# A Conformer trunk step on one core: the convolution stage's layer norms written in order with their sums on VectorE, and the last feed-forward block's first norm among the output projection's products

## The chip, the core and the metric

The kernel runs on one core of a Trainium2 chip. The metric is device time in microseconds (us) of one execution. A core has TensorE (PE, matrix products into PSUM), VectorE (DVE), ScalarE (ACT), GpSimd (POOL), and SyncE (SP), which issues most DMA transfers. Each engine runs its own queue in order and waits on semaphores for the others.

## The reference

One step of a hybrid trunk with a residual stream of 1024 features and 640 frames: 512 of a new stream and 8 x 16 of running streams. Layer 0 is a Conformer convolution module and a feed-forward block, layer 1 is chunked attention to a shared K/V and a feed-forward block, and a final RMS norm follows. Everything is float32. The parts that matter here:

```python
def layer_norm(x, g, b):
    xf = x.astype(jnp.float32)
    mu = jnp.mean(xf, axis=-1, keepdims=True)
    var = jnp.mean(jnp.square(xf - mu), axis=-1, keepdims=True)
    y = (xf - mu) * lax.rsqrt(var + EPS)
...
def swiglu_ffn(h, g, w_in, w_out):
    a, b = jnp.split(rms_norm(h, g) @ w_in, 2, axis=-1)
    return h + (jax.nn.silu(a) * b) @ w_out
...
    y = lax.conv_general_dilated(
...
    y = jax.nn.silu(layer_norm(y, ln_g, ln_b))
    return h + y @ w_pw2 + b_pw2, full[:, -CONV_HIST:]
...
            h = h + o @ w_o[j]
        h = swiglu_ffn(h, norm_ffn[l], w_ffn_in[l], w_ffn_out[l])
```

The convolution is depthwise, 31 frames wide.

## The kernel before

**Layout.** Features lie on the 128 partitions, in 8 tiles (KT), and frames along the free axis, in two groups of 320 (g = 0 and 1; 256 and 384 around attention). A float32 product is made of three fast ones: each operand is split into a high and a low part (ACT rounds the high part, VectorE subtracts), and PE multiplies high by high, low by high and high by low (mm3, L179 to L181). Weights come by DMA into `raw` and are split in the same way (wsplit, `whi` at L152, `wlo` at L156).

**Convolution stage.** It follows PLAN, a string of steps. `a`, `b`, `D` and so on to `F` are products of a channel block with its gate. `S`, `A` and `B` are depthwise convolutions of a block on PE (conv_pe, L804): 32 matmul instructions for each of the three parts of a block's frames; four of them, one `tg`, are called a step below. `q` is a block whose convolution is 31 taps, each an ACT product (`cvt`, L777) and a POOL add (`ca`, L780); further blocks are taps on VectorE (L769). Convolutions leave PSUM by a copy to `y` on ACT (to_y, L738). The inputs of S and A (`xa`) go from `gall`, which the gates on VectorE write (L724, L730), by DMA to DRAM and back, shifted (conv_shift, conv_read). The steps `n0` and `n1` are the layer norms of the two groups, LN0 and LN1 (conv_ln, L823), `w0` and `w1` the second pointwise product (pw2, L848) of the groups, whose results are added to `h` on VectorE (L862).

**Norms.** Sums over features are column sums on PE: a matmul of a data tile with a column of 1/1024 (colmean, L216). The first LCUT or SQCUT of the eight tiles are added up beforehand (L207, on POOL or VectorE) and go to PE as one; the others go to PE singly. A small reduction (L220), eps (L250) and a power of -1/2 on POOL (L257) follow, and PE spreads the result over the partitions by the identity (spread, L228). LN0 adds five of eight tiles for its mean, and none of its squares; LN1 adds five and eight.

**Feed-forward.** ffn() (L299) makes seven products where a plain scheme has eight; its first three hidden tiles are plain products (std) of the input's quarters: X11 and X21 for the first half of the frames, XT4 and X22 for the second. Each half has its norm: stats(half) (L551) makes squares (ACT, L188), sums, the spread and a copy on ACT (L554), xnorm multiplies (VectorE, L558), xput splits (ACT L337, VectorE L338). The products stand at L404. FFN0 is the block of layer 0, FFN1 that of layer 1.

**Output projection.** halves(r) (L1221) makes the products of the last heads: for each half of the frames eight tiles of six products, in PSUM tiles `mm` and `am` by turns, each added to `h` on VectorE (L1230).

**What sets the order.** A scheduler orders each engine's instructions by priority; tc.high_priority lifts what is inside, and behind(...) and tc.issue_after(...) make an instruction stand after a given one. What is written without such ties may be moved forward into gaps.

## Time and profile before

| | |
|---|---|
| median of 3 runs | 1491.54 us (1490.59 to 1494.51) |
| profiled execution | 1494.89 us |
| its span | 1493.1 us |
| mean granted TensorE clock | 0.988 |
| PE, VectorE, ACT, POOL busy | 97%, 75%, 51%, 22% of the span |

The profiled execution is one run and lies 3.35 us above the median of the runs, so sums are made against 1494.89 and carried over as differences. Times in the rows are us from the start of the span; `[3.00 <-ACT y L738]` means that the engine was idle for 3.00 us and that ACT's instruction at line 738 ended it. A matmul on f32 operands (convolutions, column sums, spreads) leaves two records for each instruction.

### The profile page before, as it was taken

Reading aid. Unit: us, or ns where it says so; the run is one execution under the profiler, and the core shown is the slowest. Engines: PE = TensorE matmul, PEld = TensorE weight load, DVE = VectorE, ACT = ScalarE, POOL = GpSimd, SP = SyncE. Lnnn points to the kernel's source line nnn. Section 1 sums busy time; section 2 is a strip of 40 time slices with the busy share of each in tenths; the row PEclk is TensorE's granted clock in tenths of the full one; section 3 lists DMA queues with packets and bytes.
Section 4 is the critical chain, followed back from the end, with each engine's and each line's share of the span. In section 5 each row is a group of like instructions: output and inputs, shape, how many; then the busy total and the mean of one; then the engine's idle time right before and its main releaser. Section 6 shows DMA issues by size and latency. Waiting matters only on the chain.

```text
span 1493.1 us, 28157 instructions
## 1 busy us (share of the span) xinstructions
PE 1443.9 (97%) x10998; PEld 1377.0 (92%) x10998; DVE 1125.9 (75%) x2494; ACT 757.4 (51%) x1620; POOL 325.5 (22%) x376
## 2 busy tenths in 40 slices
PE   5998999999999999999999999999999999999997
PEld 5997789999999999999988898878999999999997
DVE  5788546799788788766867668576788888788754
ACT  3666246464554554444655355443454455465443
POOL 5789322011111111013222111012001111111101
PEclk9999999999999999999999999999899999999998
DMA  7167514034544544424555554452024544544512
GB/s 238 67 169 199 117 57 140 31 101 121 156 110 118 153 112 116 145 86 157 195 175 193 178 193 163 142 186 78 29 75 118 148 117 115 151 117 108 157 58 71
DMA packets 66661, 192.57 MB, mean 129 GB/s; under 512 B 12000, under 2 KB 30176, under 8 KB 58080
## 3 DMA queue, kind: packets, MB, share of 16 engines
q1 hardware_dynamic: 52736, 161.10, 33.2%
q0 software_dynamic: 13504, 29.37, 9.7%
q8 instruction: 86, 1.41, 0.4%
q14 instruction: 47, 0.39, 0.1%
q10 hardware_dynamic: 288, 0.31, 0.1%
HBM read 179.14 MB, written 11.61 MB: 128 GB/s over the span
## 4 chain that ended last, share of the span: by engine, by line
PE 81%; POOL 6%; DVE 6%; ACT 4%; DMA 1%; issue 1%; POOLq 0%; DVEq 0%; ACTq 0%
PE mm L404 48%; PE mm L179 8%; PE mm L180 7%; PE mm L181 7%; POOL ca L780 5%; PE mm L818 2%; PE w L216 2%; PE am L1154 1%; PE w L1170 1%; PE am L1137 1%; ACT whi L144 1%; PE am L1201 1%; DVE wlo L338 1%; ACT whi L152 1%; DVE hid L558 1%
## 5 line engine op out<-in xcount | busy, mean ns | idle before, releaser
L404 PE MATMUL mm<-XH,whi 128*128 128x320 f32 x896 | 276.0, 311 | 1.1 <-ACT t L414 1.0
L404 PE MATMUL mm<-XH,wlo 128*128 128x320 f32 x896 | 277.0, 310 | 0.0
L404 PE MATMUL mm<-XL,whi 128*128 128x320 f32 x896 | 274.7, 309 | 0.0
L337 ACT ACTIVATE whi<-raw 128x512 fp32r<-128x512 f32 (+2 forms) x280 | 169.4, 613 | 146.2 <-PE mm L404 114.5
L179 PE MATMUL mm<-xh,whi 128*128 128x320 f32 (+2 forms) x640 | 201.0, 316 | 4.2 <-ACT xh L168 2.6
L338 DVE TENSOR_TENSOR wlo<-raw,whi 128x512 fp32r<-128x512 f32 (+2 forms) x280 | 184.9, 668 | 22.8 <-ACT whi L337 21.6
L180 PE MATMUL mm<-xh,wlo 128*128 128x320 f32 (+2 forms) x640 | 199.7, 313 | 0.6 <-DVE wlo L156 0.6
L181 PE MATMUL mm<-xl,whi 128*128 128x320 f32 (+2 forms) x640 | 196.8, 312 | 0.0
L404 PE MATMUL mm<-hid,whi 128*128 128x320 f32 x732 | 172.0, 310 | 2.9 <-DVE hid L338 2.6
L404 PEld LDWEIGHTS mm<-XH,whi 128*128 128x128 f32 x896 | 168.4, 189 | 2.1 <-ACT t L414 2.1
L404 PEld LDWEIGHTS mm<-XH,wlo 128*128 128x128 f32 x896 | 168.7, 188 | 0.0
L404 PEld LDWEIGHTS mm<-XL,whi 128*128 128x128 f32 x896 | 167.9, 188 | 0.0
L404 PEld LDWEIGHTS mm<-hid,whi 128*128 128x128 f32 x732 | 124.8, 188 | 5.8 <-DVE hid L338 3.7
L179 PEld LDWEIGHTS mm<-xh,whi 128*128 128x128 f32 x640 | 121.5, 190 | 7.4 <-ACT xh L168 3.1
L180 PEld LDWEIGHTS mm<-xh,wlo 128*128 128x128 f32 x640 | 121.7, 190 | 1.0 <-DVE wlo L156 0.8
L181 PEld LDWEIGHTS mm<-xl,whi 128*128 128x128 f32 x640 | 120.6, 189 | 0.4 <-issue 0.2
L404 PE MATMUL mm<-hid,wlo 128*128 128x320 f32 x366 | 112.9, 308 | 0.0
L404 PE MATMUL mm<-XH,shi 128*128 128x320 f32 x344 | 107.2, 312 | 3.2 <-ACT XH L337 3.2
L404 PE MATMUL mm<-XL,shi 128*128 128x320 f32 x344 | 106.8, 312 | 1.3 <-DVE XL L338 1.3
L404 PE MATMUL mm<-XH,slo 128*128 128x320 f32 x344 | 106.9, 311 | 0.0
L383 POOL DMA_DIRECT2D s<-in_w_in x38 | 22.0, 579 | 388.8 <-DVE wlo L338 208.6
L780 POOL TENSOR_TENSOR ca<-ca,cvt 128x512 f32<-128x512 f32 x60 | 91.4, 1524 | 15.0 <-ACT cvt L777 8.0
(245 smaller groups left out, 3389.1 us busy)
## 6 DMA issues: line engine op xcount, KB each, us to landing
raw<-in_w_in SPq DMA_DIRECT2D x38, 1024.0 KB
s<-in_w_in POOLq DMA_DIRECT2D x76, 256.0 KB, 4.2
raw<-in_w_os SPq DMA_DIRECT2D x24, 768.0 KB
cache<-in_ck SPq DMA_DIRECT2D x32, 512.0 KB
cache<-in_cv SPq DMA_DIRECT2D x32, 512.0 KB
raw<-in_w_pw SPq DMA_DIRECT2D x12, 1024.0 KB
s<-in_w_os POOLq DMA_DIRECT2D x48, 192.0 KB, 3.6
raw<-in_w_kq SPq DMA_DIRECT2D x8, 1024.0 KB
```

What stands on the lines that cost most here:

```text
L144: nc.scalar.activation(out=hi[:, a:b], in_=raw[:, a:b], func=AF.Copy, scale=gain)
L152: nc.scalar.activation(out=hi[:, a:b], in_=raw[:, a:b], func=AF.Copy)
L179: nc.tensor.matmul(ps, wh, xh, start=(i == 0), stop=False)
L180: nc.tensor.matmul(ps, wl, xh, start=False, stop=False)
L181: end = nc.tensor.matmul(ps, wh, xl, start=False, stop=(i == last))
L216: nc.tensor.matmul(st[:, 512 + t * w + k:513 + t * w + k], s[:, a:a + P], onec, start=True, stop=True)
L337: nc.scalar.activation(out=hi, in_=src, func=AF.Copy)
L338: put_end[0] = nc.vector.tensor_tensor(out=lo, in0=src, in1=hi.bitcast(F32), op=sub).ins
L383: nc.gpsimd.dma_start(s1, src[:, 2 * n:3 * n])
L404: last = nc.tensor.matmul(pt, wt, v, start=(first and k == i == 0), stop=(k == n - 1 and i == 2), skip_group_check=True)
L780: nc.gpsimd.tensor_tensor(out=acc, in0=acc, in1=pr, op=ALU.add)
L818: nc.tensor.matmul(pt[32 * q:32 * q + 32, 0:n], w4[0:r, 4 * tg + q, :], mv, start=(tg == 0), stop=(tg == 7))
```

## The change

**Convolution stage.** The step `n` writes LN0 in pieces among the last convolutions, each tied behind the other: mean sums, one step of B5, the spread; then subtractions, squares and adds against 12 steps, the variance sums, two steps, the spread, and the rest (staged_ln, GAPS). All adds of LN0 and LN1 are on VectorE. LN0's mean adds seven of eight tiles (LCUT) and its variance all eight squares. LN1 (step `m`) is written before w0 and tied behind LN0's last add. The first two tiles of pw2 take turns by k. QHELD takes the last two taps of channel block 3 from where they stood and issues them after the next gate (step `e`).

On PE, from LN0's mean sums on (L216 and L221 are column sums, L228 and L233 spreads, L818 and L832 convolutions of B5, B6 and B7), before:

```order
L216 MATMUL w_233_1985<-onec,acc_1986 128x1 x3
L216 MATMUL w_233_1985<-onec,y_102 128x1 x7
L818 MATMUL mm_2101<-xb_1371,w_177_1242 32x320 x3
L216 MATMUL w_233_1985<-onec,y_102 128x1 x2
L818 MATMUL mm_2101<-xb_1371,w_177_1242 32x320 x18
L228 MATMUL w_233_1985<-ident,mst_2003 128x128 x3
L818 MATMUL mm_2101<-xb_1371,w_177_1242 32x320 x11
L818 MATMUL mm_2140<-xb_1574,w_193_1377 32x320 x13
L216 MATMUL w_237_2018<-onec,sql_2017 128x1 x24
L818 MATMUL mm_2140<-xb_1574,w_193_1377 32x320 x19
L818 MATMUL mm_2174<-xb_2135,w_212_1614 32x320 x3
L228 MATMUL w_237_2018<-ident,rst_239_2054 128x128 x3
```

and with the change:

```order
L221 MATMUL w_233_1985<-onec,acc_1986 128x1 x3
L221 MATMUL w_233_1985<-onec,y_102 128x1 x3
L832 MATMUL mm_2002<-xb_1365,w_175_1236 32x320 x4
L233 MATMUL w_233_1985<-ident,mst_1999 128x128 x3
L832 MATMUL mm_2002<-xb_1365,w_175_1236 32x320 x28
L832 MATMUL mm_2070<-xb_1568,w_191_1371 32x320 x20
L221 MATMUL w_238_2019<-onec,acc_2022 128x1 x3
L832 MATMUL mm_2070<-xb_1568,w_191_1371 32x320 x8
L233 MATMUL w_238_2019<-ident,rst_243_2096 128x128 x3
L832 MATMUL mm_2070<-xb_1568,w_191_1371 32x320 x4
L832 MATMUL mm_2156<-xb_2065,w_210_1608 32x320 x32
L221 MATMUL w_255_2191<-onec,acc_2192 128x1 x3
```

The 24 sums of single squares (`sql`) became three, and each of the norm's steps stands at a fixed place. Further on, LN1's last spread stood 39 products ahead of the first product of w1; now it is four.

ACT's queue around the copy of B4 (`y_103<-mm_1579`, with the change `y_103<-mm_1573`; `cvt` are the taps of block 3, `t` the gate), before:

```order
L777 ACTIVATE cvt_1222<-gall,dwv 128x512
L777 ACTIVATE cvt_1225<-gall,dwv 128x512
L777 ACTIVATE cvt_1228<-gall,dwv 128x512
L738 ACTIVATE y_103<-mm_1579,vec 128x320
L720 ACTIVATE t_219_1674<-mm_1622,hb_87 128x320
L717 ACTIVATE t_218_1672<-mm_1647,hb_87 128x320
L738 ACTIVATE y_102<-mm_1718,vec 128x128
```

and with the change:

```order
L155 ACTIVATE whi_1611<-raw_1610 128x2048
L785 ACTIVATE cvt_1219<-gall,dwv 128x512
L785 ACTIVATE cvt_1222<-gall,dwv 128x512
L747 ACTIVATE y_103<-mm_1573,vec 128x320
L729 ACTIVATE t_217_1668<-mm_1616,hb_87 128x320
L726 ACTIVATE t_216_1666<-mm_1641,hb_87 128x320
L785 ACTIVATE cvt_1712<-gall,dwv 128x512
L785 ACTIVATE cvt_1715<-gall,dwv 128x512
L747 ACTIVATE y_102<-mm_1718,vec 128x128
```

The last two taps moved from ahead of the copy to behind the two activations of the gate.

**FFN1's first norm.** The last block of the output projection yields after each tile. After the first eight, the squares of `h`'s first half go to one tile `sqs` (ACT) and are added on VectorE (L1357); three tiles into the second half follow the column sums (L1364), eps (L1366), the power on POOL (L1368) and, at five tiles, the spread; ACT copies it to `bw` (L1374), which ffn takes in place of stats(0). The second half's norm, stats(1), is written after the second hidden tile rather than the first, tied behind that tile's third product and the split of X21.

PE at the end of the projection, with the first product of FFN1 (L404, L409) in the last row, before:

```order
L181 MATMUL am_11964<-olo_11470,whi_11855 128x320
L216 MATMUL w_1494_12050<-onec,acc_12053 128x1 x3
L216 MATMUL w_1494_12050<-onec,sq_12072 128x1 x3
L179 MATMUL am_11980<-ohi_11053,whi_11855 128x320
L180 MATMUL am_11980<-ohi_11053,wlo_11856 128x320
L181 MATMUL am_11980<-olo_11054,whi_11855 128x320
...
L181 MATMUL mm_11972<-olo_11470,whi_11855 128x320
L181 MATMUL am_11980<-olo_11470,whi_11855 128x320
L228 MATMUL w_1494_12050<-ident,rst_1505_12085 128x128 x3
L404 MATMUL mm_12128<-XH_1467_12008,shi_12033 128x320
```

and with the change:

```order
L183 MATMUL mm_11942<-ohi_11455,wlo_11842 128x320
L184 MATMUL mm_11942<-olo_11456,whi_11841 128x320
L1364 MATMUL w_1454_11950<-onec,sqs_11910 128x1 x3
L182 MATMUL am_11956<-ohi_11039,whi_11841 128x320
...
L184 MATMUL mm_11964<-olo_11456,whi_11841 128x320
L233 MATMUL w_1454_11950<-ident,sqs_11910 128x128 x3
L182 MATMUL am_11976<-ohi_11039,whi_11841 128x320
...
L184 MATMUL am_11992<-olo_11456,whi_11841 128x320
L409 MATMUL mm_12098<-XH_1470_12020,shi_12045 128x320
```

Sums of nine instructions became three, and the spread stands three tiles of six products before the projection's end. Further on, the spread of stats(1) had 67 products behind it ahead of the first product on XT4; now it is six.

The core of the diff:

```diff
+MEAN_AT, SPREAD_AT, STATS1_AT = 3, 5, 2
...
-CUT, LCUT, SQCUT = 8, (5, 5), (1, 8)
+CUT, LCUT = 8, (7, 5)
+GAPS = 1, 12, 2
+QHELD = 2
...
-        "S7 A7 n0 B5 L7 B6 B7 s0 n1 w0 w1")
+        "S7 A7 n s0 m w0 w1")
...
+            if b0 is None:
+                stats(0)
             xnorm(x11, 0, 0)
             xput(X11, x11)
-            xnorm(x21, 0, 4)
+            with tc.issue_after(put_end[0]):
+                xnorm(x21, 0, 4)
             xput(X21, x21)
+        ends, x21_end = [], put_end[1]
...
+            if jj == (b0 is not None):
                 with tc.high_priority(offset=HP):
-                    stats(1)
+                    with behind(*(() if b0 is None else (ends[STATS1_AT], x21_end))):
+                        stats(1)
...
+    def conv_pool(c):
+        acc = cp.tile([P, T], F32, tag="ca", name=nm("ca"))
+        n = W - QHELD if c else W
+        pool_taps(c, acc, range(n))
+        return (lambda: to_y(c, NB * SB, T, acc, func=AF.Copy),
+                lambda: pool_taps(c, acc, range(n, W)))
...
+            r, v = colmean(mu, [lambda c=c: y[g][:, c, :] for c in order], n, LCUT[g], "mst",
+                           nc.vector)
...
+        conv_end[0] = mean_end[0]
+        yield
+        end = spread(mu, r, n, True)
         for c in order:
             nc.vector.tensor_tensor(out=y[g][:, c, :], in0=y[g][:, c, :], in1=mu[:, :n],
                                     op=ALU.subtract)
         sq = xp.tile([P, KT, n], F32, tag="xl1", name=nm("sql"))
-        bc, _ = rstd_bc([y[g][:, c, :] for c in order], n, SQ, SQCUT[g],
-                        sqs=[sq[:, i, :] for i in range(KT)])
+        conv_end[0] = end
+        pieces = [lambda c=c, i=i: square(y[g][:, c, :], n, "a", sq[:, i, :])
+                  for i, c in enumerate(order)]
+        st = w2t()
+        hold = []
+        acc = None
+        for i in range(KT):
+            s = pieces[i]()
+            if i == 0:
+                prev = s
+                continue
+            if acc is None:
+                acc = tp.tile([P, tw[0]], F32, tag=sqt[1], name=nm("acc"), bufs=sqt[2])
+            sum_end[0] = nc.vector.tensor_tensor(out=acc[:, :n], in0=prev, in1=s, op=ALU.add).ins
+            prev = acc[:, :n]
...
+        r, v = colmean(st, [lambda: prev], n, 1, "rst", nc.vector)
+        nt = len(tiles(n))
+        nc.vector.tensor_scalar(out=r[:, :nt], in0=v, scalar1=EPS, scalar2=None, op0=ALU.add)
+        r2 = tp.tile([P, 4], F32, tag="rst2", name=nm("rst2"))
+        nc.gpsimd.tensor_tensor(out=r2[:, :nt], in0=r[:, :nt], in1=mhalf[:, :nt], op=ALU.pow)
+        conv_end[0] = mean_end[0]
+        yield
+        conv_end[0] = spread(st, r2, n, True)
...
+    def last_convs():
+        yield from conv_pe(5, "B")
+        x4s[7][2] = x4s[7][2]()
+        yield from conv_pe(6, "B")
+        yield from conv_pe(7, "B")
+
+    def staged_ln():
+        ln, convs = conv_ln(0), last_convs()
+        for gap in GAPS + (None,):
+            with tc.issue_after(conv_end[0]):
+                next(ln, None)
+            with tc.issue_after(conv_end[0]):
+                for _ in convs if gap is None else range(gap):
+                    if gap is not None:
+                        next(convs)
...
+            both = m2 == M2[0][0] and g == 0
+            for ks in [range(k, k + 1) for k in range(KT)] if both else [range(KT)]:
+                for i in range(2):
+                    mm3(pair[i], [(wh[:, (i * 8 + k) * P:(i * 8 + k + 1) * P],
+                                   wl[:, (i * 8 + k) * P:(i * 8 + k + 1) * P]) for k in ks],
+                        xk(z, ks), ks[0] == 0, ks[-1] == KT - 1)
...
+            with tc.issue_after(glu_end[0]):
+                pool_rest.pop()()
...
+    fin = halves(3, (mmt, amt), adds)
+    for _ in range(KT):
+        next(fin)
+    with tc.high_priority(offset=HP):
+        sqs = xp.tile([P, KT, 384], F32, tag="xl1", name=nm("sqs")).rearrange("p a n -> p (a n)")
+        acc, r = sqs[:, KT * NH:(KT + 1) * NH], sqs[:, (KT + 1) * NH:(KT + 1) * NH + 8]
+        for k in range(KT):
+            sq = square(h[:, k, 0:NH], NH, "a", sqs[:, k * NH:(k + 1) * NH])
+            if k:
+                sq_end = nc.vector.tensor_tensor(out=acc, in0=acc if k > 1 else sqs[:, 0:NH],
+                                                 in1=sq, op=ALU.add).ins
+    for _ in range(MEAN_AT):
+        next(fin)
+    with tc.issue_after(half_end[0]), tc.high_priority(offset=HP):
+        st, nt = w2t(), len(tiles(NH))
+        for t, c in enumerate(tiles(NH)):
+            end = nc.tensor.matmul(st[:, 512 + t:513 + t], acc[:, c:c + P], onec, start=True,
+                                   stop=True)
+        nc.vector.tensor_scalar(out=r[:, 0:nt], in0=st[:, 512:512 + nt], scalar1=EPS, scalar2=None,
+                                op0=ALU.add)
+        nc.gpsimd.tensor_tensor(out=r[:, 4:4 + nt], in0=r[:, 0:nt], in1=mhalf[:, :nt], op=ALU.pow)
+    for i in range(MEAN_AT, SPREAD_AT):
+        with tc.issue_after(end.ins):
+            next(fin)
+    with tc.issue_after(half_end[0]), tc.high_priority(offset=HP):
+        end = spread(st, r[:, 4:8], NH, True)
+        nc.scalar.activation(out=bw, in_=st[:, :NH], func=AF.Copy)
+    for i in range(SPREAD_AT, KT):
+        with tc.issue_after(end):
+            next(fin)
+    next(fin, None)
     at.close()
     early.close()
 
     hf = ExitStack()
     spare, last_add, last_mm = ffn(1, w_in1, w_out1, w_os1, ((256, 384), (0, 256)), hf,
-                                     [(split_end[0], adds[m]) for m in (1, 3, 5, 7)] + [(adds[m],) for m in (9, 11)])
+                                     [(split_end[0], i) for i in (adds[1], adds[3], adds[5], sq_end)] +
+                                     [(sq_end,), (adds[11],)],
+                                     b0=bw)
```

93 lines of the change are left out of this document (49 added, 44 removed).

## The prediction

> **What bounds the kernel now.** I read the page first, then the granted clock, then the rows around each place that the change touches.
>
> ```profile
> PE 1443.9 (97%) x10998; PEld 1377.0 (92%) x10998; DVE 1125.9 (75%) x2494; ACT 757.4 (51%) x1620; POOL 325.5 (22%) x376
> PE 81%; POOL 6%; DVE 6%; ACT 4%; DMA 1%; issue 1%; POOLq 0%; DVEq 0%; ACTq 0%
> ```
>
> TensorE is busy for 97% of the span and holds 81% of the chain that ended last. Time can come only from fewer PE instructions, from its few waits, or from stretches at a lower clock. The list of waits (us in total, times, longest) for 140 to 300 us and, third row, for 980 to 1120 us:
>
> ```profile
> PE mm L818 <- ACT y L738: 3.0, 1, 3.0
> PE w L216 <- POOL acc L207: 0.8, 1, 0.8
> PE mm L404 <- ACT XH L337: 3.2, 1, 3.2
> ```
>
> Windows in both stretches (after the window and its length: PE, its weight loads, VectorE, ACT, POOL busy, with instructions; PEclk is the third value from the right):
>
> ```profile
> 149.00:153.00 4.00, 4.00 (x52) 2.74 (x45) 4.00 (x8) 0.56 (x2) 3.84 (x4) 0.57 1.06 243
> 183.00:191.00 8.00, 8.00 (x59) 4.46 (x58) 0.35 (x2) 0.19 (x1) 0.86 (x1) 0.57 0.01 2
> 199.00:227.00 28.00, 27.20 (x192) 26.94 (x191) 15.04 (x29) 9.89 (x18) 10.94 (x8) 1.00 0.23 76
> 1024.00:1040.00 16.00, 15.21 (x108) 14.94 (x107) 12.78 (x22) 8.04 (x16) 8.95 (x8) 1.00 0.60 154
> 1047.00:1061.00 14.00, 12.82 (x51) 12.45 (x52) 12.19 (x33) 5.86 (x12) 0.00 (x0) 0.51 0.23 76
> ```
>
> In the first, second and last, TensorE counts as busy nearly throughout but is granted little more than half its clock. So the change acts on the bound: on waits, column sums and slow stretches in two short parts of the program.
>
> **Conv stage, the wait at A5.** The order of PE work there (f32 matmuls give two records each):
>
> ```profile
> 143.13 1.96 PE L818 MATMUL mm<-xa,w 128*32 128x128 f32 x64
> 148.09 4.14 PE L818 MATMUL mm<-xa,w 128*32 128x192 f32 x64 [3.00 <-ACT y L738]
> ...
> 159.68 8.92 PE L818 MATMUL mm<-xa,w 128*32 128x128 f32 x256
> 168.53 0.83 PE L216 MATMUL w<-onec,acc 128*128 128x1 f32 x6
> 169.22 1.70 PE L216 MATMUL w<-onec,y 128*128 128x1 f32 x14
> ...
> 175.74 3.44 PE L818 MATMUL mm<-xb,w 128*32 128x320 f32 x48
> 179.11 6.40 PE L216 MATMUL w<-onec,sql 128*128 128x1 f32 x48
> 185.44 5.84 PE L818 MATMUL mm<-xb,w 128*32 128x320 f32 x44
> 191.21 0.93 PE L228 MATMUL w<-ident,rst 128*128 128x128 f32 x6
> 192.07 4.50 PE L818 MATMUL mm<-xb,w 128*32 128x320 f32 x58
> ...
> 197.19 1.48 PE L216 MATMUL w<-onec,y 128*128 128x1 f32 x12
> ```
>
> and what stood ahead of that copy in ACT's queue:
>
> ```profile
> 145.56 0.72 ACT L777 ACTIVATE cvt<-gall,dwv 128x512 f32<-128x512 f32 x1 [2.32 <-POOL ca L780]
> 146.90 0.72 ACT L777 ACTIVATE cvt<-gall,dwv 128x512 f32<-128x512 f32 x1 [0.62 <-POOL ca L780]
> 147.53 0.51 ACT L738 ACTIVATE y<-mm,vec 128x320 f32<-128x320 f32 x1
> ```
>
> The two taps wait for POOL; behind them stands the copy that frees B4's PSUM buffer for A5. QHELD moves them behind the copy and the next gate's two activations. The copy can then run near 143.3 (145.56 less the 2.32 of idle), before S5 ends at 145.09, so the 3.00 go. At full clock A5 takes about 2.5 (8.92 less twice 1.96, halved) rather than 4.1, the clock being down after the wait, and F7's first two products save 0.12 each: **4.8 us**. The taps only move later; POOL's channel is read much later, at LN0's mean. Late next may be S7's shifted input, which hangs on the gate on VectorE, and this moves only about 2.7 earlier, VectorE's taps being busy till then: up to 2 us may be given back. Ends 2.8 and 4.8; I take the upper, since S7's input then comes 0.5 to 1 us from when PE wants it, on either side.
>
> **Conv stage, LN0.** From 168.53 to the first pw2 product at about 198.5 (197.19 and 1.48, less the overlap of the rows) are 30.0 us, in which PE does 192 convolution records, LN0's sums, two spreads, and nine of LN1's sums. Column sums cost about 0.12 a record (169.22 to 170.85, 14 records); convolution 0.0717 (3.44 over 48), but 0.133 (5.84 over 44) after the 48 sum records. In the new order: 12 records of mean sums 1.5; 192 convolution records at 0.0717, 13.8; two spreads of 0.86 (191.21 to 192.07) 1.7; six records of variance sums 0.7; LN1's 18 records 2.1. Sum 19.8. Onto this come waits, for which VectorE's rows matter:
>
> ```profile
> 162.21 2.29 DVE L156 TENSOR_TENSOR wlo<-raw,whi 128x2048 fp32r<-128x2048 f32 x1 [0.37 <-ACT whi L152]
> 175.92 3.27 DVE L832 TENSOR_TENSOR y<-y,w 128x320 f32<-128x320 f32 x8 [2.69 <-PE w L228]
> 186.01 0.86 POOL L257 TENSOR_TENSOR rst<-rst,mhalf 128x3 f32<-128x3 f32 x1 [12.81 <-DVE rst L250]
> ```
>
> One 128x320 operation on VectorE is 0.41 (3.27 over 8). LN0's six adds (2.5) follow the split of the weights, which ends at 164.50 less the 2.7: about 164.3, PE being there at 163.6, so 0.7. The chain under the 12 steps (96 records, 6.9 us) is eight subtractions and seven adds, 15 x 0.41 = 6.2, with hand-overs 6.4: just covered; without cover each late 0.41 is PE idle. The two steps ahead of the spread are 1.15 against eps, pow 0.86 and hand-overs, 1.4: 0.3. With 0.3 at the first spread the stretch is 21.1: **8.9 us** gained, ends 5.5 (every one of those waits a microsecond longer and one slow window) and 9.8.
>
> **LN1.** Its adds on VectorE end the 0.8 wait for POOL. But its last spread now has four products behind it before pw2's second group begins, where 39 stood. The chain behind the old spread:
>
> ```profile
> 224.13 0.83 PE L228 MATMUL w<-ident,rst 128*128 128x128 f32 x6
> 226.62 0.45 ACT L168 ACTIVATE xh<-cvt 128x320 fp32r<-128x320 f32 x1
> 228.65 1.69 DVE L169 TENSOR_TENSOR xl<-cvt,xh 128x320 fp32r<-128x320 f32 x4
> ```
>
> The first high part is ready 2.9 after the spread's start, the first low part 4.9. PE is there after 1.2, waits 1.7, does eight products (1.2) and waits 0.8 again: 2.5 of new wait, net **-1.7 us**; ends -0.5 and -6 (the clock falling in these gaps as well).
>
> **FFN1's first norm.** Before:
>
> ```profile
> 1033.79 0.31 PE L180 MATMUL am<-ohi,wlo 128*128 128x320 f32 x1
> ...
> 1036.58 0.31 PE L181 MATMUL am<-olo,whi 128*128 128x320 f32 x1
> 1037.68 0.83 PE L216 MATMUL w<-onec,acc 128*128 128x1 f32 x6 [0.80 <-POOL acc L207]
> ...
> 1043.97 0.83 PE L228 MATMUL w<-ident,rst 128*128 128x128 f32 x6
> 1047.99 0.64 PE L404 MATMUL mm<-XH,shi 128*128 128x320 f32 x1 [3.20 <-ACT XH L337]
> 1048.42 0.47 PE L404 MATMUL mm<-XH,slo 128*128 128x320 f32 x1
> ...
> 1060.93 0.30 PE L404 MATMUL mm<-XL,shi 128*128 128x320 f32 x1
> ```
>
> A product is 0.147 apart at full clock (19 steps to 1036.58) and 0.27 at half (1048.42 and its next); the clock is whole again at 1060.93, when 32 FFN1 products and 18 records of the second norm's sums are done. New: the second half began at 1032.3 (30 products before 1036.73); three blocks of six end at 1034.97. The column sums wait for VectorE, which was busy for 12.78 of 16 us from 1024 on and gets seven adds more, 2.9: a wait between 0 and 2.9, and I take the middle, 1.5, to 1036.5. Sums 0.7, two blocks 1.8: 1039.0. eps stands behind two weight splits on VectorE, pow (0.86 above) follows: 1.1, between 0 and 2. Spread 0.6, three blocks 2.65: 1043.4. The copy, the norm's multiplies and the first high parts fit into those 2.65 and the low parts come within the first eight products, so FFN1 starts unstopped; 32 products 4.7 and the moved sums 2.2 end at 1050.3. **10.6 us** gained.
>
> A wait takes some of it back. The second norm now starts later: six products stand behind its spread before its result is read, where 67 did.
>
> ```profile
> 1067.68 0.83 PE L228 MATMUL w<-ident,rst 128*128 128x128 f32 x6
> 1069.02 3.79 DVE L558 SCALAR_TENSOR_TENSOR hid<-h,vec,hid 128x320 f32<-128x320 f32 x8 [2.63 <-ACT hid L554]
> 1073.53 0.49 DVE L338 TENSOR_TENSOR XL<-hid,XH 128x320 fp32r<-128x320 f32 x1
> ```
>
> High part 2.4 after the spread, low part 6.7 (5.85, its own 0.4 and a gate's product of 0.48 now ahead of it); PE is there after 1.5, waits 0.9, does twelve products (1.8), waits 2.5: **-3.5 us**. This part is 7.1 net; ends 0 and 10.
>
> **Sum.** 4.8 + 8.9 - 1.7 + 7.1 = 19.1. The profiled execution took 1494.89 (span 1493.1 and 1.8 around it) and would take 1475.8; it stands 3.35 above the median of the runs, 1491.54, so the median comes to 1472.4; I say **1473**, as small hand-overs are missing. SP's queue is unchanged and POOL's only loses adds; what FFN0 and attention do later simply moves.
>
> **Clock: row against rule.** After 3.00 us of idle the clock fell at 149; at 1040 it fell after 0.80 idle and 18 sum records, at 183 after 48 sum records and no idle at all. So column sums seem to keep it no better than idling. My new gaps are at most 2.5 us of idle, or 2.2 of idle and sums together; LN1's 0.8 of idle with six sum records, inside 199 to 227, left it at 1.00. [...]
>
> **Rivals.**
> - *FFN1's part pays nothing.* Sums and waits at 1035 to 1040 halve the clock as they did, for 50 products at 0.12 more each, 6.0, and the 2.5 gap costs a slow window, 1.7: the 7.1 go, 1480. For it: the dip at 1040 began with less idle. Against: 18 products stand between the gaps. 0.2.
> - *VectorE is late in the conv stage.* Its queue is in written order, 6.4 against 6.9 us of cover; late by 1 at each of three places, and one slow window of 3.4 (1.7), with S7 late by 2: 6.7 less, 1480. 0.14.
> - *The conv gain is not carried*: FFN0 waits for weights instead. Its rows show no wait on a DMA in 140 to 300. It leaves 7.1: 1484. 0.05.
> - *Slower:* the clock falls at LN1's gap and does not come back through pw2's second group, as at 1047 to 1061, where sums between products kept it down; FFN0's own sums stand in that group. 192 products x 0.12 = 23, and some 58 of FFN0 7 more: 1503. It is slower only from about 200 products at half clock on. 0.07.
>
> **How the numbers follow.** The forecast (1466 to 1477) has 0.49. What is left, 0.05, is several losses together, about no change; 0.3%, 4.5 us, is about what a measurement here can tell. The range to the first two rivals and the upper ends of the gains: 1465 to 1486. Faster 0.49 + 0.2 + 0.14 + 0.05 = 0.88, same 0.05, slower 0.07.
>
> **What would show it.** No wait for ACT's y copy near 145 and clock 1.0 there; one stretch of 21 us from LN0's mean sums to pw2 without a dip; waits of 1.7 and 0.8 behind LN1's spread; the first FFN1 product within 0.5 us of the last projection block; 0.9 and 2.5 behind the second norm's spread. Wrong would be: half clock at any of those gaps, or VectorE ending its square adds over a microsecond after PE stands there.

## The result, and the profile after

The changed kernel takes 1486.91 us (median; 1483.01 to 1496.37) against 1494.21 us (1490.59 to 1500.27) of the kernel before on the same chip. The ratio is 0.9951, with a 95% interval of 0.9939 to 0.9963: faster by 7.3 us, where the prediction had 18.5. Its absolute time misses by 13.9 us; 2.7 of these are the starting point, since the three runs shown before the change (median 1491.54) were on the low side of that kernel's runs. The profiled execution took 1485.55 us, its span is 1483.6 and its mean granted clock 0.992 (before: 1493.1 and 0.988).

The page of the changed kernel, its busy time and its chain that ended last:

```profile
PE 1429.4 (96%) x10932; PEld 1365.9 (92%) x10932; DVE 1138.3 (77%) x2523; ACT 757.2 (51%) x1620; POOL 297.7 (20%) x356
PE 77%; DVE 8%; POOL 6%; ACT 3%; DMA 3%; issue 3%; SPq 0%; POOLq 0%; DVEq 0%; ACTq 0%
```

TensorE has 66 records fewer and is still what everything hangs on, but the chain now holds 3% of DMA, where it held 1%. The lists of waits (us in total, times, longest) say where. For 140 to 300 us:

```profile
PE mm L832 <- DMA xa<-sa: 6.1, 1, 6.1
PE mm L409 <- DVE XL L343: 2.9, 2, 2.2
PE mm L182 <- ACT xh L171: 1.6, 1, 1.6
PE w L221 <- DVE acc L867: 0.7, 1, 0.7
PE mm L182 <- DVE h L924: 0.5, 1, 0.5
```

and for 980 to 1120 us:

```profile
PE mm L409 <- DVE XL L343: 2.0, 1, 2.0
PE w L1364 <- DVE sqs L1357: 1.0, 1, 1.0
PE mm L409 <- ACT XH L342: 0.7, 1, 0.7
```

The wait of 3.0 for ACT's copy `y` at A5 and the wait of 3.2 for ACT's `XH` at FFN1 are gone, as forecast. The first line is new: a wait of 6.1 us for a DMA, the shifted input (`xa`) of the convolution S7, in a stretch that showed no wait on a DMA before. The second holds another new one, 2.2 us in FFN0, which the forecast does not have at all. The order of PE work from S6 to the second pointwise product (start, length, count of records, idle time before it and what ended it):

```profile
155.02 4.57 PE L832 MATMUL mm<-xa,w 128*32 128x128 f32 x128
165.72 6.77 PE L832 MATMUL mm<-xa,w 128*32 128x128 f32 x128 [6.13 <-DMA xa<-sa]
172.43 0.83 PE L221 MATMUL w<-onec,acc 128*128 128x1 f32 x6
...
182.81 0.83 PE L221 MATMUL w<-onec,acc 128*128 128x1 f32 x6 [0.74 <-DVE acc L867]
...
185.01 0.94 PE L233 MATMUL w<-ident,rst 128*128 128x128 f32 x6 [0.15 <-POOL rst L874]
...
191.55 1.48 PE L221 MATMUL w<-onec,y 128*128 128x1 f32 x12
```

S6 with A6 takes 4.57 us for 128 records; S7 with A7, the same work, takes 6.77, the clock having fallen to 0.50 at 163.48, in the wait ahead of it, until 170.31. LN0 itself went as written: from its mean sums at 172.43 to pw2's first product at 192.89 are 20.5 us, where 30.0 were (33.3 in before_again below, with more of it at half clock) and 21.1 were forecast. But these sums start 3.9 us later than before (168.53), where the forecast had them 4.8 earlier. In FFN1, the windows from 1030 to 1078 us of before and of after (clock third from the right):

```profile
1030.00:1078.00 48.00, 43.82 (x257) 42.99 (x257) 34.42 (x80) 20.58 (x44) 7.40 (x6) 0.82 0.23 71
```

```profile
1030.00:1078.00 48.00, 44.00 (x298) 42.23 (x297) 39.02 (x93) 21.72 (x46) 0.89 (x1) 1.00 0.23 72
```

In the same 48 us PE now gets 298 records done instead of 257, at a clock of 1.00 instead of 0.82. The first product of FFN1 follows the projection's last (1043.49) without a wait:

```profile
1043.63 0.31 PE L409 MATMUL mm<-XH,shi 128*128 128x320 f32 x1
```

### The profile page after: what moved, and what is told of

Its sections match the earlier page's. It is cut to its first block, busy times and chain, and to the rows that moved or that the text cites. A ratio compares the mean times of both kernels' runs of the same rounds, so it can differ in the third digit from the quotient of the medians.

```text
span 1483.6 us, 28030 instructions
## 1 busy us (share of the span) xinstructions
PE 1429.4 (96%) x10932; PEld 1365.9 (92%) x10932; DVE 1138.3 (77%) x2523; ACT 757.2 (51%) x1620; POOL 297.7 (20%) x356
## 4 chain that ended last, share of the span: by engine, by line
PE 77%; DVE 8%; POOL 6%; ACT 3%; DMA 3%; issue 3%; SPq 0%; POOLq 0%; DVEq 0%; ACTq 0%
PE mm L409 46%; PE mm L182 8%; PE mm L183 7%; PE mm L184 7%; POOL ca L788 5%; PE am L1226 1%; PE am L1209 1%; PE w L221 1%; PE w L1242 1%; ACT whi L147 1%; PE am L1273 1%; DVE wlo L343 1%; PE mm L832 1%; DVE B L446 1%; PE w L1185 1%
## 5 line engine op out<-in xcount | busy, mean ns | idle before, releaser
L409 PE MATMUL mm<-XH,wlo 128*128 128x320 f32 x896 | 276.9, 310 | 0.0
L409 PE MATMUL mm<-XH,whi 128*128 128x320 f32 x896 | 276.1, 311 | 0.7 <-ACT t L419 0.5
L409 PE MATMUL mm<-XL,whi 128*128 128x320 f32 x896 | 274.4, 310 | 0.0
L409 PE MATMUL mm<-hid,whi 128*128 128x320 f32 x732 | 171.4, 310 | 2.2 <-DVE hid L343 2.2
L409 PEld LDWEIGHTS mm<-XH,whi 128*128 128x128 f32 x896 | 168.4, 189 | 2.1 <-ACT t L419 1.3
L409 PEld LDWEIGHTS mm<-XH,wlo 128*128 128x128 f32 x896 | 169.0, 189 | 0.0
L409 PEld LDWEIGHTS mm<-XL,whi 128*128 128x128 f32 x896 | 167.9, 188 | 0.0
L409 PEld LDWEIGHTS mm<-hid,whi 128*128 128x128 f32 x732 | 124.8, 188 | 4.2 <-DVE hid L343 3.2
L409 PE MATMUL mm<-hid,wlo 128*128 128x320 f32 x366 | 112.9, 308 | 0.0
L409 PE MATMUL mm<-XL,shi 128*128 128x320 f32 x344 | 105.5, 308 | 5.0 <-DVE XL L343 5.0
L409 PE MATMUL mm<-XH,shi 128*128 128x320 f32 x344 | 105.8, 308 | 0.7 <-ACT XH L342 0.7
L409 PE MATMUL mm<-XH,slo 128*128 128x320 f32 x344 | 105.7, 307 | 0.0
```

The costliest lines, as they stand in the source:

```text
L409: last = nc.tensor.matmul(pt, wt, v, start=(first and k == i == 0), stop=(k == n - 1 and i == 2), skip_group_check=True)
```

## The experiments

All kernels below compute the whole of the reference. Every run gives its span and its mean granted clock. The product of the two is the time that the same clock cycles, idle ones included, would take at full clock; span less product is what the half clock cost. This table has the ratios, each to runs of the kernel before on the same chip, with their 95% intervals, and the means of clock and product (for the kernel before and the changed kernel over all their runs, the others over their own):

| kernel | ratio | clock | span x clock, us |
|---|---|---|---|
| before | 1 | 0.9876 | 1475.0 |
| changed | 0.9951 [0.9939, 0.9963] | 0.9921 | 1473.9 |
| conv_only | 0.9969 [0.9954, 0.9983] | 0.9895 | 1473.9 |
| ffn_only | 0.9961 [0.9947, 0.9975] | 0.9914 | 1476.7 |
| held_only | 1.0005 [0.9990, 1.0021] | 0.9882 | 1476.2 |
| taps_back | 0.9925 [0.9908, 0.9942] | 0.9930 | 1473.5 |
| norms_only | 0.9970 [0.9955, 0.9984] | 0.9891 | 1472.2 |
| late_raw | 0.9909 [0.9893, 0.9926] | 0.9947 | 1473.8 |
| no_tie | 0.9940 [0.9918, 0.9961] | 0.9929 | 1473.3 |
| repaired | 0.9912 [0.9894, 0.9931] | 0.9953 | 1472.8 |
| late_and_no_tie | 0.9920 [0.9897, 0.9943] | 0.9945 | 1472.1 |
| sums7 | 0.9918 [0.9896, 0.9940] | 0.9955 | 1473.3 |

The last column hardly moves, 1472 to 1477 in all of them. Before, the span is 1493.5 on average and the half clock costs 18.5 us; after, 1485.7 and 11.8. Of the 7.8 us between these means, 6.7 are clock and 1.1 are cycles: PE takes about as many cycles as before, waits included. In every profile the last 6 to 9 us of the span are at half clock with PE all but done, so some 3 to 5 us of both costs are the program's end and not lost. The clock is recorded in steps of 0.001, about 1.5 us, so a product is good to about one.

### The two parts alone

conv_only has the conv stage's part and both feed-forward blocks as before; ffn_only the reverse.

```diff
 # conv_only, against the changed kernel
-            if b0 is None:
-                stats(0)
+            stats(0)
...
-            with tc.issue_after(put_end[0]):
-                xnorm(x21, 0, 4)
+            xnorm(x21, 0, 4)
```

```diff
 # ffn_only, against the changed kernel
-        "S7 A7 n s0 m w0 w1")
+        "S7 A7 n0 B5 L7 B6 B7 s0 n1 w0 w1")
...
-CUT, LCUT = 8, (7, 5)
-GAPS = 1, 12, 2
-QHELD = 2
+CUT, LCUT, SQCUT = 8, (5, 5), (1, 8)
```

> The change's convolution part alone, the feed-forward blocks as before. Theory 1 (the shift copies set the pace: the wait at A5 had only hidden that S7's input comes late, and what LN0 gains is given back there, at LN1's late spread and at FFN0's second norm): ratio to before 0.998 to 1.002, with a wait of PE for the shifted input xa of 4 to 8 us before S7. Theory 2 (the 6.1 us at S7 are an accident of the profiled execution): ratio 0.994 to 0.997, and a wait there under 3 us.

> The change's feed-forward part alone (norm of FFN1 among the projection's products, late stats(1), and the ties in ffn, which FFN0 uses too). Theory 1: ratio 0.992 to 0.995, about 8 to 11 us, nearly the whole gain; first FFN1 product within 0.3 us of the last projection product, clock 1.0 from 1030 to 1070. Theory 2: ratio 0.997 to 0.999. If FFN0's new wait of 2.2 us comes from the tie in ffn it is here too; if it comes from an earlier FFN0, it is not.

Measured: 0.9969 and 0.9961, about 4.6 and 5.8 us, where the forecast's terms were 12.0 (4.8 + 8.9 - 1.7) and 7.1. So most of what is missing is missing in the conv stage. Neither run met one of its two theories whole: conv_only has the wait of the first and the ratio of the second, and ffn_only lies between the two ratios. conv_only waits 4.5 us at S7; ffn_only keeps A5's 3.0 and has the 2.2 of FFN0, so that wait comes from the feed-forward part.

### The held taps

held_only is the kernel before with QHELD alone; taps_back is the changed kernel without it; norms_only is conv_only without it.

```diff
 # held_only, against the kernel before
+QHELD = 2
...
+        n = W - QHELD if c else W
+        pool_taps(c, acc, range(n))
...
+            with tc.issue_after(glu_end[0]):
+                pool_rest.pop()()
```

```diff
 # taps_back, against the changed kernel; norms_only, against conv_only
-QHELD = 2
+QHELD = 0
```

> The kernel before with nothing but the move of the last two taps behind the gate (QHELD = 2). Theory 3 (this move alone is a loss or nothing: it brings S5 to F7 forward by the 3 us of the wait, and PE then stands before S7 for a shifted input that comes no sooner): wait at A5 gone, wait for xa before S7 of 3 to 6 us, ratio to before 0.999 to 1.003. Rival (the move is worth its wait): ratio 0.996 to 0.998.

> The changed kernel with QHELD = 0: the last two taps of block 3 stand ahead of B4's copy again. Theory 1: the wait of 3.0 us at A5 is back, the one at S7 falls by about as much (to 3 us or less), and the time is within 2 us of the changed kernel (ratio to before 0.994 to 0.9965). Theory 2: nothing falls at S7, the time is 4 to 5 us above the changed kernel (ratio 0.998).

> The conv stage's norms alone: QHELD 0 and no change in the feed-forward blocks. If the norms in written order carry what the prediction gave them (8.9 less 1.7) and the held taps cost, as the pair of taps_back and the changed kernel says (0.0026 of the time), this is 0.994 to 0.996, better than the 0.9969 of conv_only; A5 waits 3.0, S7 about 1, pw2 starts near 189, FFN0's first product near 255. Rival: the held taps cost only together with the feed-forward part, and the ratio is 0.9969 or above.

The waits of 140 to 300 us, held_only first, then taps_back:

```profile
PE mm L824 <- DMA xa<-sa: 4.9, 1, 4.9
PE mm L405 <- DVE XL L339: 1.3, 2, 0.7
PE w L217 <- POOL acc L208: 0.8, 1, 0.8
```

```profile
PE mm L832 <- ACT y L747: 3.0, 1, 3.0
PE mm L409 <- DVE XL L343: 2.9, 2, 2.2
PE mm L182 <- ACT xh L171: 1.6, 1, 1.6
PE mm L832 <- DMA xa<-sa: 1.0, 1, 1.0
```

Held taps take the 3.0 at A5 away and put 4.9 at S7. LN0's sums start at 171.54 in held_only and at 168.53 before: 3.0 later, not 4.8 earlier. In taps_back the wait at A5 came back and the one at S7 fell to 1.0, as its first expectation had it, but the time fell below both expected ranges. In none of four pairs with and without QHELD does the move gain: 1.0005 against 1; 0.9951 against 0.9925; 0.9969 against 0.9970; 0.9920 against 0.9912. In the second pair it costs 0.0026, and the intervals just touch. The first of norms_only's expectations fell: without the taps the conv part is no better than with them, so that they cost something is not shown; that they gain nothing near 4.8 us is.

Part of why S7's input is late is seen in SP's queue. SP before, and then after (start, length of the issuing, transfer):

```profile
140.91 0.34 SPq L794 DMA_DIRECT2D sb<-gall  x1
144.42 0.35 SPq L141 DMA_DIRECT2D raw<-in_w_pw  x1
144.88 2.12 SPq L800 DMA_DIRECT2D xb<-sb  x4
...
151.60 0.34 SPq L794 DMA_DIRECT2D sa<-gall  x1
155.10 1.74 SPq L800 DMA_DIRECT2D xa<-sa  x4
```

```profile
141.94 0.38 SPq L808 DMA_DIRECT2D sb<-gall  x1
144.57 0.35 SPq L144 DMA_DIRECT2D raw<-in_w_pw  x1
148.29 1.74 SPq L814 DMA_DIRECT2D xb<-sb  x4
...
151.42 0.38 SPq L808 DMA_DIRECT2D sa<-gall  x1
156.05 3.47 SPq L814 DMA_DIRECT2D xa<-sa  x4
```

In the changed kernel SP stands still for 3.3 us ahead of the `xb` copies, until `sb` has landed (`SPq L814 <- DMA sb<-gall: 3.3, 1, 3.3`); they now go out 6.4 us after `sb`, where it was 4.0 and SP's waits there show none for `sb`. `sa`, behind them, goes out 0.2 earlier than before, although the gate that it reads ends at 147.47 rather than 151.57; and `xa` goes out 0.95 later and takes twice as long to issue (1.74, as before, in after_again below, whose wait is shorter by about as much). PE, which reached S7 at about 164.1 before (half of the 8.92 us row at 159.68), is there at 159.6 and gets the input at 165.72. The order in the queue is not the whole cause, though. In held_only `sa` is not held up:

```profile
148.08 0.38 SPq L800 DMA_DIRECT2D sa<-gall  x1
154.85 1.74 SPq L806 DMA_DIRECT2D xa<-sa  x4
```

It goes out 3.5 earlier than before, and `xa` only 0.25 earlier, 6.8 us after `sa` instead of 3.5; in after_again the two are 6.05 apart. SP issues nothing else in between. SP waits 3.1 us at this place for `sa` to land in the profile before and 4.2 in the one after; that the landing of `sa` fills the longer gap of these two runs as well is an estimate from that. In the changed kernel the DMA engines were nearly full meanwhile; windows of before and after, DMA share second from the right:

```profile
142.00:166.00 24.00, 21.00 (x385) 18.35 (x387) 18.88 (x43) 9.64 (x21) 15.18 (x10) 0.93 0.66 164
```

```profile
142.00:166.00 24.00, 17.87 (x322) 15.90 (x324) 20.23 (x49) 9.68 (x21) 12.10 (x8) 0.95 0.95 227
```

The share is 0.95 of all sixteen engines' time where it was 0.66. A load of weights goes out ahead of `xb` in both kernels (144.42 and 144.57); the next `sb` and the next load come 2.2 and 3.7 us earlier with the change (159.62 and 160.81, before 161.86 and 164.53), right behind `xa`.

### The loads out of the way

late_raw is the changed kernel with the loads of pw2's third and fourth pair of output tiles tied behind S7's copies.

```diff
+            end = nc.sync.dma_start(x4[32 * s:32 * s + 32, :, 0:n - s],
+                                    sc[:, s:n].rearrange("(q p) w -> p q w", q=4)).ins
...
-                pws[KT, m2] = wsplit(w_pw2[m2], 16, P, pool=PL2[g])
+                pws[KT, m2] = wsplit(w_pw2[m2], 16, P, pool=PL2[g],
+                                     aft=xa_end[0] if g == 0 and m2 in (2, 3) else None)
```

> The changed kernel with the two loads of 1 MB of pw2 weights (third and fourth pair) tied behind the copies of S7's input on SP's queue. Theory 1 as contention (DMA engines were busy throughout from 142 to 166 us): the wait at S7 falls from 6.1 to 2 us or less and the clock stays up there; 4 to 8 us faster than the changed kernel (ratio to before 0.990 to 0.993). Theory 1 as latency (the copies' own way through DRAM and their place in SP's queue): the wait stays at 4 us or more, ratio 0.9945 to 0.996.

Its wait at S7, its SP rows, and its window:

```profile
PE mm L837 <- DMA xa<-sa: 2.1, 1, 2.1
```

```profile
150.19 0.38 SPq L809 DMA_DIRECT2D sa<-gall  x1
154.01 1.74 SPq L817 DMA_DIRECT2D xa<-sa  x4
155.85 0.38 SPq L145 DMA_DIRECT2D raw<-in_w_pw  x1
```

```profile
142.00:166.00 24.00, 21.27 (x409) 18.88 (x411) 20.77 (x51) 10.61 (x22) 12.67 (x8) 1.00 0.84 207
```

With a DMA share of 0.84, `xa` goes out 2.0 earlier and in half the time, S7 waits 2.1 instead of 6.1, the clock stays at 1.00, and the ratio is 0.9909 [0.9893, 0.9926], clear of the changed kernel's 0.9951. In the table its product is the changed kernel's; the gain is clock. The load of 144.57 now goes out at 155.85, behind `xa`, the next one stays where it was (160.54), and no work left. Issuing a load takes SP under 0.4 us. So this run shows that the load ahead of the copies lengthens their way (S7 waits 6.1 with it, 4.3 in after_again, and 2.1 without); by how much full DMA engines and by how much the waits in SP's order, it does not tell apart.

### FFN0's second norm

The tie of the multiplies `xnorm(x21, ...)` behind the first norm's split is in ffn(), which both blocks call. no_tie keeps it in FFN1 only.

```diff
-            with tc.issue_after(put_end[0]):
+            with nullcontext() if b0 is None else tc.issue_after(put_end[0]):
                 xnorm(x21, 0, 4)
```

> The changed kernel with the tie of X21's norm behind X11's split kept for FFN1 and taken off in FFN0. If the tie moved FFN0's second spread later (51 products ahead of its use before, 40 with the change), PE's wait for the low part of XT4 falls from 2.2 to about 0.6 us, and the time by 1.5 to 3.5 us: ratio to before 0.992 to 0.9945. Rival (the wait comes from FFN0's earlier start): wait 2 us, ratio as the changed kernel's, 0.995.

The second norm's spread and the first product with a low part of XT4, before and after:

```profile
281.92 0.83 PE L228 MATMUL w<-ident,rst 128*128 128x128 f32 x6
288.30 0.41 PE L404 MATMUL mm<-XL,shi 128*128 128x320 f32 x1 [0.57 <-DVE XL L338]
```

```profile
282.37 0.83 PE L233 MATMUL w<-ident,rst 128*128 128x128 f32 x6
288.76 0.41 PE L409 MATMUL mm<-XL,shi 128*128 128x320 f32 x1 [2.19 <-DVE XL L343]
```

From spread to low part are 6.4 us in both. But FFN0's first product came 1.2 us earlier (260.15, before 261.35) and the spread 0.45 later, behind more of the products: PE reaches the low part 4.2 us after the spread (288.76 less 2.19 and 282.37), where it took 5.8, and stands idle for the difference. In no_tie the wait is 0.57 again. The ratio of 0.9940 [0.9918, 0.9961] lies 1.6 us below the changed kernel's, with overlapping intervals: the wait is shown to be the tie's, its price in time is not shown beyond that.

### The clock

before_again and after_again are the two kernels once more, unchanged, for another profile of each.

> The kernel before, unchanged, for one more profile. Theory of the clock: it falls in windows of about 3.4 us whose position is not the program's, so the same gaps halve it in one execution and not in the next; half-clock time before the last 15 us differs from the 27 us of the first profile by more than 7 us, and FFN1's start shows another number than 17 us. Rival: the gaps decide alone, 27 and 17 us again, within one window each.

> The changed kernel once more, one profile, for the clock. If stretches at half clock are fixed by the gaps, the same places show it as in its first profile: 6.8 us at S7, 3.4 at the start of pw2, 3.4 behind LN1's spread, 3.4 at FFN0's second norm, 17.1 in all, and none between 1030 and 1078. If they depend on where the gaps fall in a window of fixed length that the program does not set, S7 (6.1 of idle) halves again, the gaps of 2.2 and less may or may not, and the total differs by one or two lengths of 3.4.

before_again took 1494.85 us (span 1493.0), after_again 1489.16 (1487.2, clock 0.991). The waits at S7 and in FFN0 came back:

```profile
PE mm L832 <- DMA xa<-sa: 4.3, 1, 4.3
PE mm L409 <- DVE XL L343: 2.8, 2, 2.2
```

but the half clock did not all fall in the same places. Microseconds at half clock, by part of the program (PE's idle end of the program left out):

| profile | conv stage, to 225 us | FFN0 and attention | FFN1 |
|---|---|---|---|
| before | 10.2 | 0 | 17.1 |
| before_again | 17.1 | 0 | 17.1 |
| held_only | 13.7 | 0 | 10.2 |
| conv_only | 6.8 | 6.8 | 6.8 |
| norms_only | 6.8 | 3.4 | 20.5 |
| ffn_only | 17.1 | 0 | 3.4 |
| after | 10.2 | 6.8 | 0 |
| after_again | 6.8 | 10.2 | 3.4 |
| taps_back | 0 | 6.8 | 0 |
| late_raw | 3.4 | 3.4 | 3.4 |
| no_tie | 6.8 | 0 | 0 |
| repaired | 6.8 | 0 | 3.4 |
| late_and_no_tie | 3.4 | 0 | 0 |
| sums7 | 3.4 | 3.4 | 0 |

The first five have the same code in FFN1 and show 6.8 to 20.5 us, 14.3 on average; the other nine have the new code there and show 0 to 3.4, 1.5 on average. A microsecond at half clock costs about half of one (a product takes 0.267 us there instead of 0.147, in the profiles before and after), so the new code saves about (14.3 - 1.5) / 2 = 6.4 us of clock. That the gaps alone fix the stretches held for FFN1 in before_again (17.1 again) and fell everywhere else (before_again's total, 34.1 for 27.3, differs by two lengths, a little under the 7 that its first expectation asked): the conv stage before has 10.2 and then 17.1, FFN1's old code down to 6.8, and after_again halves at FFN0's first norm and FFN1's second, where the first profile did not, and not at LN1's spread, where it did.

Every stretch in this table is 3.413 us long or a whole multiple, and within one execution all of them lie on one grid: in the changed kernel's profile they begin at 163.48, 194.20, 228.34 and 289.78, that is 9, 10 and 18 steps apart. Between executions the grid lies differently against the program: before and before_again, one kernel, have their first stretch from 149.41 and from 148.36. With the grid of each of the fourteen profiles laid over its rows from 100 to 1470 us, each window can be told by how much of it PE spent idle (the times in brackets) or on column sums (each from its start to the next start), and by the clock of the next:

| window at full clock, idle and column sums in it | windows | next one at half clock |
|---|---|---|
| under 1.5 us | 5430 | 0 |
| 1.5 to 2.0 us | 59 | 5 |
| 2.0 us and more | 45 | 44 |

Of windows with idle time alone, 2 of 8 between 1.6 and 1.8 us had a half one behind them, 24 of 24 with 2.0 and more (none lies between); with column sums alone the line is at about 2.0 (2 of 18 between 1.8 and 2.0, 13 of 14 above). A window already at half clock that held 1.0 or more of either left the next one at half, too (all 19 of them), with under 0.5 the clock returned (47 of 47), and between them in 2 of 4. Windows of the changed kernel, each with the one behind it (PE busy first, clock third from the right):

```profile
190.80:194.20 3.40, 3.40 (x31) 3.34 (x28) 1.65 (x4) 3.40 (x9) 0.00 (x0) 1.00 0.00 0
194.20:197.60 3.40, 3.40 (x15) 3.40 (x14) 1.79 (x4) 2.09 (x6) 0.00 (x0) 0.50 0.00 0
...
286.40:289.80 3.40, 1.21 (x9) 1.04 (x8) 3.40 (x9) 3.07 (x8) 0.00 (x0) 1.00 0.00 0
289.80:293.20 3.40, 3.40 (x15) 3.40 (x14) 3.40 (x10) 0.68 (x2) 0.00 (x0) 0.50 0.00 0
...
1071.40:1074.80 3.40, 1.58 (x11) 1.58 (x12) 3.40 (x10) 2.73 (x7) 0.00 (x0) 1.00 0.01 2
1074.80:1078.20 3.40, 3.40 (x26) 3.40 (x25) 3.40 (x9) 0.25 (x2) 0.00 (x0) 1.00 0.02 5
```

The first holds LN1's 18 column-sum records: busy throughout, and the next is at half. The third holds all of FFN0's 2.19 of idle, and the next is at half. The fifth holds 1.79 of the 2.04 that the second norm of FFN1 waits, and nothing happens; in after_again the grid put 2.02 of it into one window, and there the clock fell. In the fourteen profiles a window with 2.0 us of idle in it was always enough (24 of 24), and so, nearly, were column sums (13 of 14).

### Together

repaired is the changed kernel with QHELD = 0, late_raw's tie and no_tie's. late_and_no_tie differs from it in QHELD = 2 only. sums7 is repaired with seven of LN1's eight tiles added on VectorE.

```diff
 # sums7, against repaired
-CUT, LCUT = 8, (7, 5)
+CUT, LCUT = 8, (7, 7)
```

> The changed kernel with QHELD = 0, the two late weight loads and no tie in FFN0: each loss found so far taken away. If they add up (about 4 us for the taps, 2 to 4 for the loads, 2 for the tie): ratio 0.986 to 0.989, no wait for xa, the wait of 3.0 us at A5 back, 0.6 us at FFN0's second norm. Rival (taps and loads are one loss, at S7, and do not add): 0.990 to 0.992.

> The changed kernel with QHELD left at 2, the loads of pw2's third and fourth pair behind S7's copies, and the tie in the first feed-forward block taken away: it differs from the run `repaired` only in QHELD. If the held taps are worth what the prediction took once the loads stand out of the way, A5 does not wait (3.0 there), S7 waits no more than the 2.1 of `late_raw` would be without its taps, and LN0's sums start about 2 us before the 169.0 of `repaired`: ratio to the kernel before 0.988 to 0.990. If shared transfers still eat what A5 gains, as a held-up S7 did in `held_only`, S7 waits 2 or more, LN0's sums start within 1 us of 169, and the ratio is that of `repaired` within its interval, 0.990 to 0.993.

> The kernel of the run `repaired` with LN1's mean over seven of eight tiles added on VectorE instead of five: 12 column-sum records fewer ahead of and among pw2's first products, 1.4 us by the 1.48 of 12 such records in the profiles, two adds of 0.41 more on VectorE, which has 5 us of convolutions on PE to do them in. If the sums only cost their own time, the ratio is 0.990 and the place shows no new wait; if VectorE is the later one there, PE waits up to 0.8 at LN1's mean and the ratio stays 0.991 to 0.992. A stretch at half clock at the start of pw2 is expected in neither, since `repaired` had none there.

All three are at 0.991 to 0.992 and cannot be told from late_raw or from one another: 1482.08, 1481.27 and 1481.80 us. That is what repaired's rival expected: the losses at the taps and at the loads do not add up. late_and_no_tie starts LN0's sums at 166.81, 2.2 earlier than repaired's 169.03, and its A5 and S7 hardly wait for others (0.4 for the DMA, 1.6 of issue): with the loads moved, the held taps do for A5 what was forecast of them, and the runs still do not tell the two apart. In the profiles the 2.2 are there at pw2's first product too (187.28 and 189.50), 0.9 are left at FFN0's (254.34 and 255.22), 0.8 having gone to a wait of FFN0's first norm for POOL that repaired doesn't show (each of the two has one window at half clock in between), and 0.2 at FFN1's (1036.59 and 1036.78). Of its two expectations the place is nearer the first and the ratio the second. sums7 removes the column sums that had halved pw2's first window in six of the nine other profiles with this norm; no such window there, and no gain that the runs can tell. A version that is faster than both kernels is thus the changed kernel with late_raw's tie, 1483.16 us, or repaired.

## Why the prediction was wrong

- **A5, 4.8 us: this step failed.** "Late next may be S7's shifted input ... up to 2 us may be given back. Ends 2.8 and 4.8; I take the upper". The wait at A5 and the low clock behind it did go. But the input came 6.1 late (4.3 in after_again, 4.9 in held_only), not 0.5 to 1 from when PE wants it, and the clock fell with it, to 0.50 for 6.8 us. It is not the gate that was late: that came 4.1 earlier (147.47, before 151.57), more than the 2.7 reckoned with. The term is about 0 by held_only's time, and LN0's sums start 3.9 later in the changed kernel's profile; the lower end should have been below zero. What it overlooked: the prediction put SP's queue down as unchanged, and asked only when the gate ends. Ahead of the copies, in SP's order, stand others that wait for a landing (3.3 us for `sb` in the changed kernel), and a load of weights goes out ahead of them in a stretch with a DMA share of 0.95; the prediction's own row of 149 to 153 us had one of 1.06. late_raw shows that the loads are a cause: without the one ahead of the copies the wait is 2.1.
- **LN0, 8.9 us: right.** The stretch was 30.0 and is 20.5. The waits inside it, 0.74 at the variance sums and 0.15 at the spread, were forecast as "just covered" and 0.3.
- **LN1, -1.7 us: mechanism right, size too small.** The waits of 1.58 and 0.52 are the 1.7 and 0.8 forecast. But from pw2's first product to FFN0's first, 62.8 us in three of the four profiles with the old norm (65.9 in ffn_only, where 6.8 us of it are at half clock), took 65.7 at the least (taps_back, repaired) and 67.3 in the changed kernel's profile, 70.2 in after_again: -2.9 to -7.4, of which 2.1 is LN1's two waits, some 0.8 a wait of FFN0's own first norm for POOL in some of them, and the rest windows at half clock, at pw2's first products behind 18 column sums and behind LN1's or FFN0's norm. The ends given, -0.5 and -6, hold most of it; the value taken had no clock in it.
- **FFN1's first norm, 10.6 us, and its second, -3.5 us: right.** Counted from the same product of the projection, the 81st of 192, FFN1's first product came after 27.66 us before and 22.02 after, 5.6 less (forecast 4.6, to 1043.4); its 301st, behind the second norm, after 84.09 and 76.35, 7.7 less (forecast 7.1), and 6.2 less in after_again, where the second norm halved the clock. The sums wait 0.98 (forecast 1.5), the second norm 0.73 and 2.04 (forecast 0.9 and 2.5). Alone, with FFN0's wait in it, the part is worth 5.8 by ffn_only. Only the half clock that the 10.6 took away, 17.1 us, was a little more than that code's average of 14.3; that is 1.4 us of time, by the luck of that profile.
- **FFN0: a term that was missing, and failed too.** "What FFN0 and attention do later simply moves" was wrong: ffn() serves both blocks, and its tie costs FFN0 1.6 us of new wait, and a window at half clock (1.7) in four of the five profiles that have it. The rival "the conv gain is not carried", with FFN0 waiting for weights, shows in part where FFN0 starts earliest with the tie: from its first product to the projection's 81st, 759.0 us before and 761.5 after, are 767.2 in taps_back and 765.0 in late_raw, and 2.7 and 1.6 of these are a wait of PE at 594 for ACT's split of weights (`whi`). repaired, as early and without the tie, takes 759.5 and shows no wait for `whi` there; each is one profile.
- **The clock.** The sum took it that none of the new gaps halves the clock. The rule behind that is shown by no run, and it was wrong at three of the gaps forecast, in one of the changed kernel's two profiles or in both: the 18 sum records ahead of pw2, LN1's gap, and the second norm's in FFN1. The row that spoke against it stood in the prediction itself: the clock had fallen after 0.80 of idle with 18 sum records. The rivals' "slow window of 3.4 (1.7)" is in the profiles, the dip at 149 among them: 3.413 us at half clock, of which about half is lost. With the windows counted above, a gap of 2.2 us falls far enough into one window in about two executions of three (estimate: 2.2 / 3.41, if 1.7 us of idle in a window decides, where 2 of 8 did between 1.6 and 1.8 and 24 of 24 with 2.0 and more; FFN0's did in four profiles of five), and each such window costs 1.7.

Followed through the first profiles of the two kernels, the terms are these, forecast and measured: up to LN0's sums 4.8 and -3.9; LN0 8.9 and 9.5; from pw2 to FFN0 -1.7 and -4.4; from FFN0 to the projection's 81st product 0 and -2.5; FFN1 7.1 and 7.7. They add up to 19.1 and 6.4. With after_again in place of the first profile the measured ones are -1.2, 9.5, -7.4, -3.0 and 6.2, together 4.1. So the largest part of the missing 11.2 us is the step at A5, 8.7 in one profile and 6.0 in the other, then LN1 with its clock, 2.7 and 5.7, then FFN0, 2.5 and 3.0. Of the rivals, that of a late VectorE had S7 late by 2 as one of its mishaps and 1480 as its time; none had the shifted copies' way through the DMA queue as its cause, and the range ended 0.9 us below the measured median. That the clock stays down through w1, the rival that would have made it slower, did not come: a window at half clock was followed by one at full as soon as it held under 0.5 us of idle and sums (47 of 47).

## What to carry to other kernels

When a wait in front of PE goes, follow the next input back through its transfers to the queue that issues them: what stands ahead of it there, what that waits for, and how full the DMA engines are in that stretch. A mean granted clock below 1 hides time that no list of waits shows (18.5 us at 0.9876 here); count idle time and column sums per window of the length that the profiles show (3.413 us here), keep each window below what halved the next one (here none of 5430 with under 1.5 us of them did, 5 of 59 from 1.5 to 2.0, 44 of 45 with more), and price a longer gap by its chance of falling into one window, from more than one profile. A helper that two blocks share moves both when one is changed.

## What the runs showed that was not expected

- Nearly all of the gain is clock: span times granted clock is 1475.0 us before and 1473.9 after, while the half clock's cost went from 18.5 to 11.8 us.
- In each of the fourteen profiles the stretches at half clock lie on one grid of 3.413 us, and the grid lies differently from one execution to another (149.41 and 148.36 for the first stretch of the same kernel). A window with 2.0 us or more of idle time or 128x1 matmuls halved the next one in 44 of 45 cases, one with under 1.5 in none of 5430. Column sums, matmuls of the form 128x1, counted here as idle time did (13 of 14 windows with 2.0 us of them alone), however busy the row looks.
- In a window already at half clock 1.0 us of either was enough to leave the next one at half (all 19 of them); with that, several short gaps at FFN1 kept it down for up to 20.5 us (norms_only, in two stretches).
